# Hybrid attention and gating trunk: gating's output products moved behind attention, one PSUM sum per token tile and column half

## Chip, cores and metric

The kernel runs on one core of one Trainium2 chip. The metric is the device time of one execution in microseconds (us), as the median of several runs. All engines of the core work at once: PE (matrix products; PEld is its weight load), DVE (VectorE), ACT (ScalarE), POOL (GpSimd) and SP (SyncE, which here only issues DMAs).

## What is computed

Two layers over 512 latent and 256 context tokens with 1024 features. The change lies in layer 0, the hybrid layer. There a normalised and modulated input `h` is projected to q, k, v (8 heads of 64) and to u, g of a spatial gating unit (512 features). The mixer's output is one product over 1024 features, of which 512 come from attention and 512 from gating:

```python
q, k, v, u, g = jnp.split(h_lat @ w_in, splits, axis=-1)
a_lat = neighbourhood_attention(heads(q), heads(k), heads(v), heads(kc), heads(vc), rpb)
s_lat = spatial_gating(jax.nn.gelu(u), jax.nn.gelu(g), w_s, b_s)
y_lat = jnp.concatenate([a_lat, s_lat], axis=-1) @ w_out
```

The same is done for the context tokens. The result is normalised (RMS), gated and added to the input; a second norm and modulation make the input of the gated MLP (ConvFFN). Layer 1 has retention in place of the hybrid mixer and a second FFN.

## The kernel before

Tokens are six tiles of 128: tiles 0 to 3 are latent, 4 and 5 context, and they are worked on in the order 4, 5, 0, 1, 2, 3 (`toks`). Every fp32 product is three fp32r matmuls on split operands (`mm3`, L128): `split` (L97) lets ACT make the high part and DVE the low part. A weight unit is 128 x 1024 (512 KB): `unit` (L101) loads it into one of three raw buffers (tag `raw`) and splits it into one of the places that `slot` hands out in turn. PSUM has eight banks of 512 columns: four with tag A, two with B and two with C (L94).

The order of instructions on each engine is made by a planner, which takes program order as its guide and moves ready work forward. Where `self.fixed` names an engine (L73, L62), its instructions stay in program order; in the opening these are PE and SP ("TQ", L708), the others are planned.

Stages of layer 0, with the names the trace shows:

- Opening (`sgu`, L708 to L766). `first_load` loads x (`xn`), `ada_first` (L176) the modulation weights of a quarter of the features (`ar`; products `ad`, turned by `adt` into columns `ab`). `first_x` (L411) computes the first norm of each tile and scales it, `first_xT` (L1731) transposes it (`ht` to `xT`, copied by ACT), `first_h` (L1741) applies the modulation and splits into `h0a` and `h1a`. `tokens(q, ...)` are the gating products (`ug`) of one quarter of the features (`ug10` to `ug13` are their weights).
- Gating (L772 to L829). The second half of the projection (`ug00` to `ug03`), the mixing over positions (`mix`), the transposes (`turn`, tiles `st0A` to `st3C`, split into `sT`), then four weight units `wos0` to `wos3` and the output products `wsg`: `out_pieces` (L588) makes 12 pieces (six tiles, two column halves of 512) of 12 matmuls each, and ACT copies each sum into `y` (name `ysg`). Background jobs (`bg`, modulation gates, tiles `ag` and `G`) are called in between.
- Attention (L831). Four pairs of heads; each pair has its projection (`project_pair`, tiles `pq`, `px`, `pk`, `pv`, `py` from weights `wq`, `wk`, `wv`), scores `s`, softmax on DVE and ACT (`sc`), transposes `pt`, and the products `o` and `oc` with the values, which end in `at`. The projection of the next pair runs as `fills`, one per step. In the last pair the fills are two pieces of the output product of tile 4 with the features of pairs 0 and 1 (`woa0`, `woa1`; `wata`). `bias_tiles` loads each head's bias (`slab`) and makes `tm`.
- End of attention (L884 to L897). The weights `woa2`, `woa3`; then `watb` (tile 4 with pairs 2 and 3, 12 matmuls) and `watc` (the other five tiles with all four pairs, 12 matmuls per half). DVE adds each sum to `y`. After a tile's second half, `final` calls `residual` (L425): squares (`jyb`, ACT), times the gate `G` (DVE), the root (POOL), plus the input (`xb`), squares (`jxb`), root, scaling. Then the next stage's blocks are built: transposes `ht`, `sa` (tiles 4, 5, 0) and `sb` (tiles 1, 2, 3), splits `hb` and `b`. The FFN's first products are `pf`; `pf000b` is the first on the second half's blocks.
- The FFN writes partial outputs by DMAs from POOL's queue (`yp`, `ypg` to `yd`, later `yf`).

`h0` and `h1` are tags of two SBUF places of 24 KB per partition: the high and low part of `h` until the last projection, then blocks of the FFN and (`h1`) its staging tile `sa`.

Of the kernel before, what the change touches and what calls it, by code (L numbers as in the profile page):

```python
# [18 lines left out]
KD = 8  # L19
# [49 lines left out]
class Trunk:  # L69
# [106 lines left out]
    def ada_first(self, q, pool, tag):  # L176
# [6 lines left out]
        for n in range(2):  # L183
            for kp in range(2):
# [226 lines left out]
    def first_x(self, toks, xn):  # L411
        V, G = self.V, self.G
        for t in toks:
            y = xn[t]
            junk = self.bp.tile([P, D], BF16, name=f"jx{t}", tag="t2k", bufs=4)
            ss = self.bp.tile([P, 1], F32, name=f"ssx{t}", tag="ss", bufs=8)
            if t % 2:
                V.tensor_tensor_reduce(
                    out=junk, in0=y, in1=y, scale=1.0 / D, scalar=0.0, op0=ALU.mult, op1=ALU.add, accum_out=ss
                )  # L420
            else:
                self.S.activation(junk, y, AF.Square, scale=1.0 / 32, accum_out=ss)
            V.tensor_scalar(out=y, in0=y, scalar1=self.rstd(ss, f"x0{t}"), scalar2=None, op0=ALU.mult)

    def residual(self, t, y, gate, src, last, name, xt):  # L425
# [58 lines left out]
    def alloc_blocks(self, l):  # L484
# [5 lines left out]
        self.sa = self.bp.tile([P, KD, n], F32, name=f"sa{l}", tag="h1", bufs=1)  # L490
# [133 lines left out]
    def finisher(self, gates, src, ab, name, xts, last=False, mlp=None):  # L624
# [4 lines left out]
        def fin(t, y):  # L629
# [12 lines left out]
            self.residual(t, y, gates[1 if t >= 4 else 0], src(t), last, name, xt)  # L642
# [19 lines left out]
    def sgu(self, y, xn):  # L662
        S, V, T, G, a = self.S, self.V, self.T, self.G, self.a
        toks = (4, 5, 0, 1, 2, 3)
        with ExitStack() as ctx:
# [17 lines left out]
            with ExitStack() as c2:  # L683
# [29 lines left out]
                later = self.ada_first(1, fp, "B")  # L713
                raws[1] = ug_raw(1)
                for i in range(4):
                    product(i)
                self.first_x((4, 5), xn)
                turned(0)
                turn()
                product, turn = later  # L720
                self.first_h(0, 2, xT)
                w = ug_split(0, raws[0])
                self.first_x((0, 1), xn)
                tokens(0, (4, 5))
                turned(1)
                product(0)
                product(1)
                self.first_x((2, 3), xn)
                self.first_h(0, 0, xT)
                turned(2)  # L730
                product(2)
                product(3)
                tokens(0, (0, 1))
                self.first_h(0, 1, xT)
                turn()
                tokens(0, (2, 3))
                def after(q):
                    u = ug_split(q, raws[q])
                    for chunk, ct in chunks:
                        self.first_h(q, chunk, xT)  # L740
                    return u

                w = after(1)
                product, turn = self.ada_first(2, fp, "B")
                raws[2] = ug_raw(2)
                for n, t in enumerate(toks):
# [4 lines left out]
                    if n == 1:  # L751
                        turn()
                        w2 = after(2)
# [6 lines left out]
                for n, t in enumerate(toks):  # L760
                    tokens(2, (t,))
                    if n == 0:
                        turn()
                        w3 = after(3)
# [6 lines left out]
            st = [sp.tile([P, 4, 768], F32R, name=f"sT{i}", tag=f"sT{i}") for i in range(2)]  # L771
# [30 lines left out]
            def turn(half):  # L802
                for f in (2 * half, 2 * half + 1):
                    for tt, tag in (((0, 1, 2, 3), "A"), ((4, 5), "C")):
                        n = len(tt) * P
                        pt = self.ps(f"st{f}{tag}", tag)
                        fc = slice(f % 2 * P, f % 2 * P + P)
                        for j, t in enumerate(tt):
                            T.transpose(pt[:, j * P : (j + 1) * P], u[half][:, t, fc], self.ident)
                        c = slice(tt[0] * P, tt[0] * P + n)  # L810
                        self.split(st[0][:, f, c], st[1][:, f, c], pt[:, :n])
# [12 lines left out]
            wo = [self.unit(a["hyb_out"][(4 + f) * P : (5 + f) * P], f"wos{f}") for f in range(4)]  # L824
            mix(1)
            turn(1)
            pieces = self.out_pieces([(st[0][:, f, :], st[1][:, f, :]) for f in range(4)], wo, y, toks, True, None, "sg")
            for f in pieces:
                f()  # L829

    def attention(self, y, final):  # L831
        a = self.a
        with ExitStack() as ctx:
# [15 lines left out]
            toks = (4, 5, 0, 1, 2, 3)  # L849
            for i in range(n + lag + 1):  # L850
                if i < n:
# [3 lines left out]
                    if step == 0:  # L855
                        pr["at"] = [ap.tile([P, 768], F32R, name=f"at{x}{j}", tag=f"at{x}", bufs=4) for x in range(2)]
                        if j == 3:
                            A = (
                                [pairs[0]["at"], pairs[1]["at"]],
                                [self.unit(a["hyb_out"][f * P : (f + 1) * P], f"woa{f}") for f in (0, 1)],  # L860
# [1056 lines left out]
```

## Time and profile before

| | |
|---|---|
| time, three runs | 1894.61, 1899.68, 1899.76 us (median 1899.68) |
| profiled execution | 1894.09 us, of which the span of the trace is 1892.3 |
| mean granted PE clock | 0.979 |
| opening and gating | 0 to 157.7 us |
| attention, to the last projection | 157.7 to 322.2 |
| last pair of heads | 322.2 to 360.9 |
| output products and norm | 360.9 to 400.3, then 400.3 to 419.3 |
| FFN of layer 0 and layer 1 | 419.3 to the end |
| DMA | 249.80 MB, mean 132 GB/s over the span |

The bounds of the stages are read from the first and last start of their tiles. In a table of stretches, each row has the stretch, its length, then for PE, PEld, DVE, ACT and POOL the busy time with the count of instructions, and last the granted PE clock (1.00 is full speed), the DMA engines' busy share and GB/s. In a timeline a row is: start, duration, engine, line, operation, output<-inputs, shapes, count, and in brackets the idle time before it and what ended it; all rows say L61, the helper that records every instruction, so tiles tell the place. A matmul's duration contains the pipeline's latency; the spacing of starts is what it costs PE. In a list of waits: who waited for whom, the sum, how often, and the longest, in us.

### The profile page before, as it was taken

How to read it: one execution, taken by the hardware profiler on the slowest of the kernel's cores; microseconds unless marked ns; L12 is line 12 of the kernel's file. 1: busy time of each engine (PE TensorE's matmuls, PEld its weight loads, DVE VectorE, ACT ScalarE, POOL GpSimd, SP SyncE). 2: the span in 40 equal slices, each digit the busy share in tenths (PEclk: the TensorE clock that was granted, in tenths of full speed). 3: DMA queues.
4: the chain of work that ended last, by engine and by line, in shares of the span. 5: the costliest groups of instructions: out<-in, count | busy, mean ns of one | idle time of the engine just before them, and what ended most of it. 6: DMA issues, size and time to landing. Idle time of an engine off the chain costs nothing. (4 is left out here: it accounts for less than half of the span.)

```text
span 1892.3 us, 28961 instructions
## 1 busy us (share of the span) xinstructions
PE 1796.2 (95%) x11104; PEld 1596.4 (84%) x11104; DVE 1328.8 (70%) x2250; ACT 1015.1 (54%) x1828; POOL 320.6 (17%) x451
## 2 busy tenths in 40 slices
PE   6999999879999999999889999999999989999997
PEld 4887777669989889998779989988999779899996
DVE  4532545779877878778777566676655689888987
ACT  4523455766646466565565434343444467576763
POOL 1102212120122222222121011011001110122221
PEclk9999999979999999999999999999999989999999
DMA  8323323232667768677642322431421225777772
GB/s 310 127 89 95 95 93 95 72 115 84 193 165 151 186 137 179 149 166 153 228 153 86 118 80 83 123 101 53 126 68 60 98 77 149 180 200 177 193 176 101
DMA packets 83628, 249.80 MB, mean 132 GB/s; under 512 B 10912, under 2 KB 12448, under 8 KB 83488
## 3 DMA queue, kind: packets, MB, share of 16 engines
q1 hardware_dynamic: 56960, 199.00, 32.2%
q0 software_dynamic: 25952, 48.83, 15.1%
q8 instruction: 87, 1.43, 0.3%
q14 instruction: 53, 0.43, 0.1%
q10 hardware_dynamic: 576, 0.11, 0.0%
HBM read 191.28 MB, written 39.85 MB: 122 GB/s over the span
## 5 line engine op out<-in xcount | busy, mean ns | idle before, releaser
L61 DVE SCALAR_TENSOR_TENSOR cv<-pre,cw,cv 128x769 f32<-128x769 f32 (+1 forms) x176 | 152.7, 881 | 7.7 <-ACT cv L61 7.1
L61 DVE SCALAR_TENSOR_TENSOR acc<-ar,cs,acc 128x512 f32<-128x512 f32 x160 | 118.1, 750 | 27.7 <-DMA ar<-in_adaw 18.1
L61 ACT ACTIVATE cv<-pre,cw 128x770 f32<-128x770 f32 (+1 forms) x88 | 81.1, 924 | 37.9 <-DVE pre L61 37.3
L61 POOL DMA_DIRECT2D yf<-yp x64 | 55.6, 869 | 261.9 <-ACT yp L61 159.0
L61 POOL DMA_DIRECT2D yd<-yp x54 | 46.5, 868 | 186.1 <-ACT yp L61 182.6
L61 ACT COPY yp<-wf 128x512 f32<-128x512 f32 x118 | 67.9, 577 | 17.6 <-PE wf L61 17.3
L61 ACT ACTIVATE pre<-px 128x256 f32<-128x256 f32 (+2 forms) x160 | 54.3, 366 | 40.0 <-PE px L61 39.6
L61 POOL DMA_DIRECT2D yd<-ypg x54 | 44.7, 850 | 158.4 <-ACT ypg L61 150.1
L61 POOL TENSOR_SCALAR rrr<-rmv 128x2 f32<-128x2 f32 x16 | 3.0, 190 | 360.9 <-DVE rmv L61 360.9
L61 ACT ACTIVATE g<-cv 128x770 fp32r<-128x770 f32 (+1 forms) x44 | 32.5, 738 | 29.8 <-DVE cv L61 29.7
L61 PE MATMUL px<-hs,wd 128*128 128x384 f32 x240 | 45.3, 336 | 0.0
L61 PEld LDWEIGHTS px<-hs,wd 128*128 128x128 f32 x240 | 42.4, 188 | 1.6
L61 ACT ACTIVATE pre<-py 128x384 f32<-128x384 f32 (+1 forms) x40 | 17.4, 436 | 44.5 <-DVE cv L61 28.2
L61 DVE TENSOR_TENSOR g<-cv,g 128x770 fp32r<-128x770 f32 (+1 forms) x44 | 36.2, 822 | 6.8 <-ACT g L61 6.2
L61 ACT ACTIVATE cv<-cv 128x770 f32<-128x770 f32 (+1 forms) x44 | 32.7, 742 | 12.3 <-DVE cv L61 12.1
L61 DVE TENSOR_TENSOR cv<-cv 128x770 f32<-128x770 f32 (+1 forms) x44 | 36.2, 823 | 2.4 <-ACT cv L61 1.4
L61 DVE TENSOR_TENSOR pre<-pre,pz 128x256 f32<-128x256 f32 (+1 forms) x60 | 20.9, 372 | 23.2 <-PE pz L61 23.2
L61 PE MATMUL ad<-ar,c 128*32 128x256 f32 (+1 forms) x224 | 26.7, 515 | 10.4 <-DMA ar<-in_adaw 9.8
L61 DVE CUSTOM_DVE_ANT_0 sc<-s,tm 128x256 f32<-128x256 f32 x32 | 13.4, 420 | 32.6 <-PE s L61 23.5
L61 ACT ACTIVATE sc<-sc,sst 128x512 f32<-128x512 f32 x32 | 23.2, 725 | 23.1 <-DVE sc L61 20.7
L61 PEld LDWEIGHTS px<-hs 128*128 128x128 f32 x240 | 30.8, 190 | 5.5 <-DVE pre L61 4.5
L61 POOL TENSOR_TENSOR tm<-slab,mask 128x256 f32<-128x256 f32 (+1 forms) x32 | 24.4, 793 | 65.2 <-DVE sst L61 65.0
(2617 smaller groups left out, 6852.9 us busy)
## 6 DMA issues: line engine op xcount, KB each, us to landing
ar<-in_adaw SPq DMA_DIRECT2D x96, 512.0 KB, 4.2
yf<-yp POOLq DMA_DIRECT2D x64, 256.0 KB, 4.1
yd<-yp POOLq DMA_DIRECT2D x54, 256.0 KB, 5.1
yd<-ypg POOLq DMA_DIRECT2D x54, 256.0 KB, 4.6
fin<-xd SPq DMA_DIRECT2D x10, 512.0 KB, 7.4
xd<-xd SPq DMA_DIRECT2D x8, 512.0 KB, 3.2
xn<-in_x SPq DMA_DIRECT2D x6, 512.0 KB, 6.2
xb<-in_x SPq DMA_DIRECT2D x6, 512.0 KB, 3.6
```

What stands on the lines that cost most here:

```text
L61: r = f(*p, **k)
```

## The change

The gating unit makes no output product any more. Its transposed and split result is kept per token tile (`sT`, in the place `y{t}`). In attention, `part(t, n, fs)` adds the features `fs` (0 to 3 gating, 4 to 7 attention) for tile `t` and half `n` to one PSUM sum of tag A. Five weight units (`wo0` to `wo4`) are loaded at the last pair, three of them into the place of `h1`; twelve fills do features 0 to 4 of tiles 4 and 5. After attention `wo5` to `wo7` are loaded into places of attention's tiles (`unit_parts` is new), then each tile's sums are finished and `final` reads them in PSUM. So the copies of `wsg` and the adds of `wata`, `watb` and `watc` are gone. The staging tile `sa` gets a place of its own, and the scratch for DMAs issued by GpSimd is given as 4096 bytes to make room.

```diff
+    def unit_parts(self, src, name, pool, tags):
+        raw = self.bp.tile([P, 1024], F32, name=f"{name}r", tag="raw", bufs=3)
+        self.load(raw, src)
+        p = [pool.tile([P, 512], F32R, name=f"{name}{g}", tag=g, bufs=1) for g in tags]
+        for h in range(2):
+            self.split(p[2 * h], p[2 * h + 1], raw[:, 512 * h : 512 * h + 512])
+        return [Halves([p[i], p[2 + i]]) for i in range(2)]
...
     def residual(...)
+        if sums is None:
+            sums = [y[:, h] for h in hv]
         for n, h in enumerate(hv):
-            self.ssq(y[:, h], f"y{name}{t}", n)
-        for h in hv:
-            V.tensor_tensor(out=y[:, h], in0=y[:, h], in1=gate[:, h], op=ALU.mult)
+            self.ssq(sums[n], f"y{name}{t}", n)
+        for n, h in enumerate(hv):
+            V.tensor_tensor(out=y[:, h], in0=sums[n], in1=gate[:, h], op=ALU.mult)
...
-        self.sa = self.bp.tile([P, KD, n], F32, name=f"sa{l}", tag="h1", bufs=1)
+        self.sa = self.bp.tile([P, KD, n], F32, name=f"sa{l}", tag="sa", bufs=1)
...
             def turn(half):
-                for f in (2 * half, 2 * half + 1):
-                    for tt, tag in (((0, 1, 2, 3), "A"), ((4, 5), "C")):
...
+                for tt, tag in (((4, 5), "C"), ((0, 1), "B"), ((2, 3), "C")):
+                    pt = self.ps(f"st{half}{tt[0]}", tag, (P, 2, 2, P))
+                    for i, t in enumerate(tt):
+                        if half == 0:
+                            pool = self.bp if t < 4 else self.lp
+                            self.sT[t] = pool.tile([P, 2, 4, P], F32R, name=f"sT{t}", tag=f"y{t}", bufs=1)
+                        for f in range(2):
+                            T.transpose(pt[:, i, f, :], u[half][:, t, f * P : f * P + P], self.ident)
+                        fs = slice(2 * half, 2 * half + 2)
+                        self.split(self.sT[t][:, 0, fs, :], self.sT[t][:, 1, fs, :], pt[:, i])
...
-            wo = [self.unit(a["hyb_out"][(4 + f) * P : (5 + f) * P], f"wos{f}") for f in range(4)]
             mix(1)
             turn(1)
-            pieces = self.out_pieces([(st[0][:, f, :], st[1][:, f, :]) for f in range(4)], wo, y, toks, True, None, "sg")
-            for f in pieces:
-                f()
...
     def attention(self, y, final):
+            wo, sums = [], {}
+            row = lambda f: a["hyb_out"][(f + 4) % 8 * P : ((f + 4) % 8 + 1) * P]
+            def part(t, n, fs):
+                if fs[0] == 0:
+                    sums[t, n] = self.ps(f"wo{t}{n}", "A")
+                o = slice(512 * n, 512 * n + 512)
+                for f in fs:
+                    if f < 4:
+                        x = [self.sT[t][:, i, f, :] for i in range(2)]
+                    else:
+                        x = [z[:, self.gcol(t)] for z in pairs[f - 4]["at"]]
+                    self.mm3(sums[t, n], x, [z[:, o] for z in wo[f]], f == 0, f == 7)
...
                         if j == 3:
-                            A = (...)
-                            fills = self.out_pieces(*A, y, toks[:1], False, None, "ata", "A")
+                            home = self.bp.tile([P, 6, 1024], F32R, name="woh", tag="h1", bufs=1)
+                            for f in range(5):
+                                at_ = None if f < 2 else (home[:, 2 * f - 4], home[:, 2 * f - 3])
+                                wo.append(self.unit(row(f), f"wo{f}", at_))
+                            fills = [
+                                lambda t=t, n=n, fs=fs: part(t, n, fs)
+                                for t in toks[:2]
+                                for n in range(2)
+                                for fs in ((0, 1), (2, 3), (4,))
+                            ]
...
+            spare = ap.tile([P, 2, 1024], F32R, name="wo7s", tag="ptall")
+            wo.append(self.unit_parts(row(5), "wo5", ap, ("q0", "q1", "kb0", "kb1")))
+            wo.append(self.unit_halves(row(6), "wo6", ap, "sc", 4))
+            wo.append(self.unit(row(7), "wo7", (spare[:, 0], spare[:, 1])))
             self.early()
-            self.out_group(*B, y, toks[:1], False, final, "atb", "A")
-            self.out_group(A[0] + B[0], A[1] + B[1], y, toks[1:], False, final, "atc", "A")
+            for t in toks:
+                for m in range(2):
+                    part(t, m, range(5, 8) if t > 3 else range(8))
+                y[t] = self.ytile(t, "yat")
+                final(t, y[t], [sums[t, m] for m in range(2)])
...
-    nc = bacc.Bacc("TRN2", target_bir_lowering=False, num_devices=1)
+    nc = bacc.Bacc("TRN2", target_bir_lowering=False, num_devices=1, dynamic_dma_scratch_size=4096)
```

The opening is written in another order, and all five engines keep program order in it: `self.fixed` is "TQSVG" (PE, SP, ACT, DVE, POOL). `first_x` is divided into `first_sq` (sum of squares and root) and `first_scale`. Every second copy of `first_xT` goes to DVE. x of tiles 0 and 1 is loaded ahead of the modulation weights, and the first gating weight between their halves (`amid`):

```diff
-                self.fixed = "TQ"
-                product, turn = self.ada_first(0, fp, "C")
                 self.first_load((0, 1), xn)
-                raws = {0: ug_raw(0)}
+                product, turn = self.ada_first(0, fp, "C", lambda: later.update(w=ug_raw(0)))
                 self.first_load((2, 3), xn)
...
+                sq(4, "S")
+                sq(5, "V")
+                scale(4)
+                scale(5)
+                sq(0, "S")
+                sq(1, "V")
+                turned(0)
+                scale(0)
+                scale(1)
+                product(0)
+                product(1)
+                w = ug_split(0, raws[0])
+                turned(1)
+                product(2)
+                product(3)
+                turn()
+                self.first_h(0, 2, xT)
+                sq(2, "S")
+                self.first_h(0, 0, xT)
+                sq(3, "V")
+                scale(2)
+                scale(3)
+                tokens(0, (4, 5))
+                turned(2)
+                product, turn = ada1
+                for i in range(4):
+                    product(i)
+                self.first_h(0, 1, xT)
+                tokens(0, (0,))
+                turn()
+                w1 = ug_split(1, raws[1])
+                tokens(0, (1, 2, 3))
...
-                    if n == 1:
+                    if n == 2:
                         turn()
-                        w2 = after(2)
+                        w2 = ug_split(2, raws[2])
+                        after(2)
```

More of the change, by code (lines that the diff above doesn't have):

```diff
@@ L174, in ada_unit_src, with ada_first @@
         return self.a["adaw"][r : r + P]
-    def ada_first(self, q, pool, tag):
+    def ada_first(self, q, pool, tag, amid=None):
         S, V, T = self.S, self.V, self.T
@@ L183, in ada_first @@
         for n in range(2):
+            if n and amid:
+                amid()
             for kp in range(2):
@@ L409, in first_load, with first_sq, first_scale, residual @@
             self.load(xn[t], self.a["x6"][t * P : (t + 1) * P])
[L411 to L425, printed above, removed]
+    def first_sq(self, t, xn, engine):
+        y = xn[t]
+        junk = self.bp.tile([P, D], BF16, name=f"jx{t}", tag="t2k", bufs=4)
+        ss = self.bp.tile([P, 1], F32, name=f"ssx{t}", tag="ss", bufs=8)
+        if engine == "V":
+            self.V.tensor_tensor_reduce(
+                out=junk, in0=y, in1=y, scale=1.0 / D, scalar=0.0, op0=ALU.mult, op1=ALU.add, accum_out=ss
+            )
+        else:
+            self.S.activation(junk, y, AF.Square, scale=1.0 / 32, accum_out=ss)
+        return self.rstd(ss, f"x0{t}")
+    def first_scale(self, t, xn, r):
+        self.V.tensor_scalar(out=xn[t], in0=xn[t], scalar1=r, scalar2=None, op0=ALU.mult)
+    def residual(self, t, y, gate, src, last, name, xt, sums=None):
         V = self.V
@@ L627, in finisher, with fin @@
         state = {"n": 0}
-        def fin(t, y):
+        def fin(t, y, sums=None):
             if not done and not last:
@@ L641, in fin @@
                 state["n"] += 1
-            self.residual(t, y, gates[1 if t >= 4 else 0], src(t), last, name, xt)
+            self.residual(t, y, gates[1 if t >= 4 else 0], src(t), last, name, xt, sums)
             done[t] = y
@@ L706, in turned @@
                     self.first_xT(*chunks[n], xn, fp, xT, banks[n])
-                self.fixed = "TQ"
-                product, turn = self.ada_first(0, fp, "C")
+                self.fixed = "TQSVG"
+                r, later = {}, {}
                 self.first_load((0, 1), xn)
-                raws = {0: ug_raw(0)}
+                product, turn = self.ada_first(0, fp, "C", lambda: later.update(w=ug_raw(0)))
                 self.first_load((2, 3), xn)
-                later = self.ada_first(1, fp, "B")
+                raws = {0: later["w"]}
@@ L718, in sgu @@
-                turned(0)
+                self.first_h(0, 1, xT)
+                tokens(0, (0,))
                 turn()
[L720 to L736, printed above, removed]
+                w1 = ug_split(1, raws[1])
+                tokens(0, (1, 2, 3))
                 def after(q):
-                    u = ug_split(q, raws[q])
                     for chunk, ct in chunks:
                         self.first_h(q, chunk, xT)
-                    return u
-                w = after(1)
+                after(1)
@@ L763, in sgu @@
                         turn()
-                        w3 = after(3)
+                        w3 = ug_split(3, raws[3])
+                        after(3)
                 w = w3
@@ L770, in sgu @@
             vl = sp.tile([P, 6, 512], F32R, name="vnl", tag="vnl")
-            st = [sp.tile([P, 4, 768], F32R, name=f"sT{i}", tag=f"sT{i}") for i in range(2)]
             for t in toks:
@@ L1738, in first_xT @@
                     self.T.transpose(pt[:, i, j * P : (j + 1) * P], xn[t][:, k * P : (k + 1) * P], self.ident)
-            self.S.copy(xT[chunk][:, 2 * kk : 2 * kk + 2, :], pt)
+            if kk % 2:
+                self.V.tensor_copy(xT[chunk][:, 2 * kk : 2 * kk + 2, :], pt)
+            else:
+                self.S.copy(xT[chunk][:, 2 * kk : 2 * kk + 2, :], pt)
     def first_h(self, q, chunk, xT):
@@ L1758, in build @@
         self.sst = {}
+        self.sT = {}
         self.jobs = []
```

25 lines of the change are left out of this document (5 added, 20 removed).

## Prediction

> **What bounds the kernel.** I read the busy shares first, then who TensorE (PE) waited for up to 425 us, then the busy table of the stretches that the change touches.
>
> ```profile
> PE 1796.2 (95%) x11104; PEld 1596.4 (84%) x11104; DVE 1328.8 (70%) x2250; ACT 1015.1 (54%) x1828; POOL 320.6 (17%) x451
> PE ad L61 <- DMA ar<-in_adaw: 9.8, 4, 8.1
> PE ht L61 <- DVE ysg L61: 7.8, 2, 4.2
> PE ug L61 <- ACT h0a L61: 5.4, 1, 5.4
> ...
> 120.00:157.70 37.70, 36.90 (x160) 28.45 (x158) 7.43 (x12) 12.04 (x20) 0.00 (x0) 1.00 0.22 75
> 157.70:322.20 164.50, 157.62 (x984) 124.82 (x983) 80.40 (x226) 83.60 (x193) 35.06 (x47) 0.98 0.33 105
> 322.20:360.90 38.70, 32.46 (x248) 24.70 (x247) 29.14 (x102) 29.74 (x77) 3.67 (x5) 1.00 0.14 42
> 360.90:400.30 39.40, 35.79 (x170) 28.96 (x168) 28.16 (x47) 23.47 (x55) 9.31 (x16) 0.96 0.38 133
> 400.30:419.30 19.00, 10.54 (x50) 8.91 (x47) 13.59 (x24) 11.91 (x30) 7.16 (x13) 0.68 0.35 118
> ```
>
> PE is the bound: 95% busy, and in every stretch but the last its column is nearly the length of the stretch. So a moved matmul saves nothing by itself. The change can win only idle PE time: matmuls put where PE now waits, and waits that go. The table shows where. In the gating end (120 to 157.7) PE is full, while VectorE (DVE, 7.43) and ScalarE (ACT, 12.04) rest. Near the end of attention (322 to 361) PE has 38.70 - 32.46 = 6.2 us of holes. After it come the output products (361 to 400) and a tail to the next stage's first matmul on its second half (400 to 419), where PE is busy for 10.5 of 19 us, at a granted clock of 0.68, and waits for DVE and ACT, which run the norm of the last tokens.
>
> **Term 1, the gating end.**
>
> ```profile
> 120.31 0.48 PE L61 MATMUL wsg<-wos0h,sT 128*128 128x512 f32 x1
> ...
> 120.86 0.60 PE L61 MATMUL st3A<-ident,un 128*128 128x128 f32 x4
> ...
> 121.43 0.70 PE L61 MATMUL wsg<-wos0h,sT 128*128 128x512 f32 x2
> ...
> 129.72 0.50 PE L61 MATMUL wsg<-wos0h,sT 128*128 128x512 f32 x1 [0.22 <-ACT ysg L61]
> ...
> 157.73 0.41 PE L61 MATMUL pq<-h0a,wq0h 128*128 128x512 f32 x1
> 156.53 1.06 ACT L61 ACTIVATE wq0h<-wq0r 128x1024 fp32r<-128x1024 f32 x1 [0.80 <-PE wsg L61]
> 157.62 1.23 DVE L61 TENSOR_TENSOR wq0l<-wq0r,wq0h 128x1024 fp32r<-128x1024 f32 x1 [28.31 <-ACT wq0h L61]
> ```
>
> There are 12 pieces (6 token tiles, 2 halves) of 12 matmuls (4 features, 3 products) = 144. The last 10 pieces run from 129.72 to 157.73: 28.01 / 120 = 0.2334 us each, so 144 are 33.6 us. The whole stretch is 157.73 - 120.31 = 37.4 us. In it stay the last transposes (120.86 to 121.43, 0.6 us) and four gate products of the background job, about 1.0 us by the spacing of their neighbours. That removes 35.8. Attention's first products must then start near 122 us. Their weight takes the two splits shown (1.06 and 1.23); today its slot comes free only behind the output weights, tomorrow behind the gating weights, while the mixing products still run. I charge 1.1 us of wait (0 if the splits are ready, 4 if two units' splits queue on DVE behind the mixing). **-34.7** (-35.8 to -31.8). The 12 ACT copies that go, and the finer splits of the gating result (128x256 in place of 128x512), lie on engines idle here and are costed at nothing. If DVE were not idle, six more small splits would be some 2 us.
>
> **Term 2, the last pair of heads.** The fills grow from 2 pieces of 6 matmuls to 12 pieces with 60: five weight units for two tiles and two halves. 48 more at 0.2334 are 11.2 us of PE work.
>
> ```profile
> 321.96 0.28 PE L61 MATMUL py<-h1a,wv3h 128*128 128x256 f32 x1
> ...
> 299.75 0.33 SPq L61 DMA_DIRECT2D woa3r<-in_hyb_out  x1
> 311.42 0.63 SPq L61 DMA_DIRECT2D slab<-in_rpb  x1
> L61 POOL TENSOR_TENSOR tm<-slab,mask x32: 510/859/1567, 167.3 to 330.4; 128x256 f32<-128x256 f32 x16, 128x128 f32<-128x128 f32 x16
> ```
>
> Three of the five units (wo2 to wo4) go to the place of h1, which the projection reads until 322. So they cannot be split earlier, and their raw copies hold all three raw buffers until then. SyncE's queue would stand at the next weight load, and behind it may stand the last head's bias load (now at 311.42) and the FFN's first weight; today GpSimd makes the last tiles from it at 330.4, so a load some microseconds after 322 is still in time. The splits, 3 x 1.06 on ACT and 3 x 1.23 on DVE, come into a stretch where these engines are already busy for about 29 of 39 us and softmax passes from one to the other. Lower end: all 6.2 us of holes filled, +5.0. Upper end: nothing filled and the splits in series, 11.2 + 6.9 = +18.1. I take half of the holes, **+8.0**: the fills depend on nothing but weights, so they can run in the waits, but PE takes its queue in order.
>
> **Term 3, the output products.**
>
> ```profile
> 360.92 0.47 PE L61 MATMUL watb<-woa2h,at 128*128 128x512 f32 x1
> ...
> 367.50 0.39 PE L61 MATMUL watc<-woa0h,at 128*128 128x512 f32 x1
> ...
> 375.67 0.27 PE L61 MATMUL ht<-ident,ysg 128*128 128x128 f32 x1
> 379.56 1.52 PE L61 MATMUL ht<-ident,ysg 128*128 128x128 f32 x7 [3.61 <-DVE ysg L61]
> ...
> 388.34 1.04 PE L61 MATMUL ht<-ident,ysg 128*128 128x128 f32 x8
> 389.14 0.47 PE L61 MATMUL watc<-woa0h,at 128*128 128x512 f32 x1
> ...
> 399.46 0.85 PE L61 MATMUL watc<-woa3s,at 128*128 128x512 f32 x3
> ...
> 419.25 0.69 PE L61 MATMUL pf000b<-b,wp0h 128*128 128x384 f32 x1 [1.63 <-ACT b L61]
> ```
>
> Today 132 matmuls; afterwards 2 tiles x 2 x 9 = 36 and 4 tiles x 2 x 24 = 192, so 228. The 36 from 367.50 to 375.67 take 0.227 each: 51.7 us. Four groups of transposes (0.80 each, 388.34 to 389.14) add 3.2 and attention's last products 0.6. One wait of 1.0 is allowed: the open sums of tiles 4 and 5 hold all four banks of tag A, so tile 0 starts only when tile 4's first half is read. Together 56.5, against 39.4 now, in which the hole of 3.6 us should go: a tile now occupies PE for 48 x 0.227 = 10.9 us, about as long as its norm chain takes. **+17.1** (+16.1 without the wait; +22.8 if the hole stays, with about 2 us of slow matmuls after it). The third more weight (wo5) at the end is 0.7 us of DVE and 0.6 of ACT per half; its places (q0 to kb1) come free with the last scores, before the last products, and it is costed at nothing; uncovered it is 2.3.
>
> **Term 4, the tail.** DVE loses the adds and the norm reads the sums where they are.
>
> ```profile
> L61 DVE TENSOR_TENSOR ysg<-watc,ysg 128x512 f32<-128x512 f32 x8 | 5.5, 683 | 0.0
> L61 DVE TENSOR_TENSOR ysg<-ysg,G 128x512 f32<-128x512 f32 x8 | 5.5, 690 | 1.8 <-ACT jyb L61 1.6
> L61 ACT ACTIVATE jyb<-ysg 128x512 bf16<-128x512 f32 x9 | 5.6, 626 | 4.0 <-DVE ysg L61 4.0
> ...
> 408.27 0.61 ACT L61 ACTIVATE jyb<-ysg 128x512 bf16<-128x512 f32 x1
> ```
>
> An operand in PSUM costs nothing extra: the add reads PSUM in 683 ns, the multiply reads SBUF in 690. Two adds per tile go, 1.4 us of DVE. More important, DVE and ACT are two tiles behind when the last matmul is issued at 400 (the last tile's second sum of squares starts at 408.27) and will not be, since PE becomes the slower one. From 408.27 to 419.25 the chain of one tile takes 11.0; with the first half's square 11.6, in place of 419.25 - 400.3 = 18.9. **-7.3** (0 if the backlog stays, -8.5 with the saved multiply wait).
>
> The Trainium skill speaks against holding sums: PSUM — Partial Sum Buffer, section Summary: rules for kernel authors, says to evacuate promptly since PSUM is tight. By it this change would stall PE; that is rival (c) below. The trace of before reads each sum once, so it shows no such hold.
>
> **Term 5, the opening.**
>
> ```profile
> 15.00:20.00 5.00, 3.31 (x17) 3.04 (x15) 1.48 (x5) 4.13 (x7) 0.57 (x2) 1.00 1.03 419
> ...
> 23.71 0.79 PE L61 MATMUL ug<-ug10h,h0a 128*128 128x512 f32 x1 [5.40 <-ACT h0a L61]
> ...
> 41.93 0.39 PE L61 MATMUL ug<-ug11h,h0a 128*128 128x512 f32 x1
> ...
> 47.93 0.66 PE L61 MATMUL adt<-ident,mr 128*128 128x128 f32 x4 [0.71 <-ACT mr L61]
> ```
>
> DMA is full (419 GB/s, 1.25 us per 512 KB tile). Three tiles move ahead of the second half of the first modulation weights, which so come 3.8 us later; but the second chunk's transposes now run before that, in the 5.4 us hole. By hand I get the first gating product no earlier than now, a cold spell less, then a hole of up to 3 us before the third chunk's transposes, as VectorE, ScalarE and GpSimd wait in program order. The second quarter's products (41.93) then start about 1 us earlier, and the 0.7 us wait at 47.93 goes with the later turn. **-2** (-5 to +5).
>
> The sa tile's own place and the smaller DMA scratch are costed at nothing: no wait on h1 is listed at the start of either FFN; the scratch is the second rival.
>
> **Sum** against the profiled execution's 1894.09 us (span 1892.3): -34.7 + 8.0 + 17.1 - 7.3 - 2.0 = -18.9, so 1875.2. The runs shown before are 1894.61, 1899.68 and 1899.76, so the median lies 5.6 above the profiled one and the lowest 0.5. I add half the median's distance, 2.8: **1878**.
>
> **Rivals.** (a) *All holes fill*: terms at their good ends, -35.8 + 5.0 + 16.1 - 8.5 - 5 = -28, so 1866 to 1869. For it: DVE and ACT idle where they are charged. Against: in-order PE, late wo2 to wo4.
> (b) *The change doesn't do what it says*, the work moves and no hole fills: -34.7 + 18.1 + 22.8 + 0 - 2 = +4, so 1901. For it: the splits enter the softmax stretch. Against: fills are independent of softmax.
> (c) *Banks*: the norm holds each sum for two squares and two multiplies (about 3 us), and if PE had to wait it out for all six tiles, 18 us: 1896. Against: four banks are two tiles, 11 us of matmuls, so only the first handover should show.
> (d) *Slower*: the scratch for DMA issued by GpSimd is cut from its default to 4096.
>
> ```profile
> yd<-yp POOLq DMA_DIRECT2D x54, 256.0 KB, 5.1
> ...
> 566.38 0.86 POOL L61 DMA_DIRECT2D yd<-yp  x1 [8.10 <-ACT yp L61]
> 567.78 0.85 POOL L61 DMA_DIRECT2D yd<-yp  x1 [0.55 <-ACT yp L61]
> ...
> PE wf L61 <- ACT ypg L61: 4.6, 2, 3.2
> ```
>
> Transfers are issued 1.4 us apart and land after 5.1. If two no longer fit, the second waits 3.7 us. Over 54 such transfers that is 200 us on GpSimd; four buffers hide most, and if a sixth reaches PE (which already waits 4.6 us for ypg) it is +33: 1911. It decides from the point where two transfers don't fit; nothing in the trace shows the limit.
>
> **Chances.** Forecast 0.58 (1869 to 1888), (a) 0.20, (b) 0.10, (c) 0.05, (d) 0.07. A measurement of this kernel tells 0.3% from no change, 5.7 us around 1899.68: forecast and (a) are faster, 0.78; (b) and (c) the same, 0.15; (d) slower, 0.07. The range is 1865 to 1896: it takes in (a) to (c)'s edge and leaves out (b) and (d) and a little below.
>
> **What would show it.** Attention's first projection near 120 to 124 us; the last pair longer by about 8 us and with fewer PE holes; four output tiles about 11 us apart, without a hole of 3 us; 11 to 12 us from the last output product to the FFN's second-half product. Wrong, if PE waits for wo weights or for norm reads of the sums, if the last head's bias comes late, or if the wf products wait longer for yp and ypg.

## The result, and the profile after

The changed kernel takes **1871.61 us** (median of 4 runs, 1862.28 to 1876.50) against 1898.62 (4 runs, 1894.61 to 1899.76): a ratio of 0.9856, 95% interval 0.981 to 0.9901. Two later sets, each beside runs of the kernel before on the same chip, gave 0.9858 (0.9836 to 0.988) and 0.9865 (0.9851 to 0.9879). In microseconds the medians differ by 27.0, 27.5 and 24.9. The profiled execution is the one of 1875.21 us; its span is 1873.4.

The page of after, the line of busy times:

```profile
PE 1792.3 (96%) x11104; PEld 1596.5 (85%) x11104; DVE 1327.4 (71%) x2247; ACT 1009.4 (54%) x1815; POOL 318.8 (17%) x451
```

PE has as many instructions as before and 4 us less busy time. What the kernel won is 15 us of idle PE time in this pair of executions. The table of stretches shows where (columns: length, then busy time and instructions of PE, weight loads, DVE, ACT and POOL, then granted clock, DMA share, GB/s). After:

```profile
36.84:116.00 79.16, 79.16 (x553) 65.09 (x551) 37.70 (x73) 34.31 (x60) 8.46 (x16) 1.00 0.35 120
116.00:281.00 165.00, 159.96 (x1004) 126.40 (x1003) 82.88 (x235) 85.62 (x199) 35.14 (x47) 0.98 0.35 109
281.00:322.00 41.00, 40.41 (x272) 30.14 (x272) 32.63 (x104) 31.93 (x80) 4.77 (x5) 1.00 0.25 75
322.00:381.30 59.30, 58.80 (x282) 47.43 (x279) 29.43 (x46) 28.80 (x67) 8.67 (x20) 1.00 0.33 111
381.30:393.00 11.70, 8.34 (x52) 6.92 (x50) 7.89 (x15) 9.01 (x21) 3.79 (x9) 0.96 0.39 132
```

The last pair of heads (281 to 322) now has 0.6 us of PE holes where it had 6.2, the output products (322 to 381.3) have 0.5 where they had 3.6, and the tail is short, at a clock of 0.96 instead of 0.68: by the marks below 10.0 us in place of 19.1 (pf000b starts 1.7 us before the last row ends). The marks between the stages, from the timeline of after (start, duration, engine, operation):

```profile
113.51 0.44 PE L61 MATMUL mx<-vnh,sguwh 128*128 128x384 f32 x1
...
115.96 0.48 PE L61 MATMUL pq<-h0a,wq0h 128*128 128x512 f32 x1
...
323.08 0.66 PE L61 MATMUL pt<-ident,sc 128*128 128x128 f32 x4
...
381.24 1.03 PE L61 MATMUL ht<-ident,yat 128*128 128x128 f32 x8
...
391.26 0.44 PE L61 MATMUL pf000b<-b,wp0h 128*128 128x384 f32 x1 [1.77 <-ACT b L61]
```

The same marks of before, from its timeline, as far as the prediction doesn't show them:

```profile
117.52 0.44 PE L61 MATMUL mx<-vnh,sguwh 128*128 128x384 f32 x1
...
360.50 0.66 PE L61 MATMUL pt<-ident,sc 128*128 128x128 f32 x4
...
400.15 0.38 PE L61 MATMUL ht<-ident,ysg 128*128 128x128 f32 x2
```

Set against each other, the front of the kernel adds up as follows. "Mixing" is the first mixing product of the second half, "projection" the last of attention's projections on `h1a` (321.96 before, 280.00 after), "last tile" the transposes that end the output products.

| stage, between marks | before | after | difference | predicted |
|---|---|---|---|---|
| start to mixing (term 5) | 117.52 | 113.51 | -4.0 | -2 |
| mixing to attention's first product (1) | 40.2 | 2.45 | -37.8 | -34.7 |
| to the last projection | 164.2 | 164.0 | -0.2 | 0 |
| to pt of the last head tile (2) | 38.5 | 43.1 | +4.5 | +8.0 |
| to the last tile (3) | 39.65 | 58.16 | +18.5 | +17.1 |
| to pf000b (4) | 19.1 | 10.0 | -9.1 | -7.3 |
| **sum at pf000b** | 419.25 | 391.26 | **-28.0** | -18.9 |
| from pf000b to the end | 1473.05 | 1482.1 | +9.1 | 0 |

The two spans differ by 18.9 us, exactly the predicted sum. That is a coincidence: the front won 9 us more than predicted and the part behind it lost 9. The experiments had two questions: is this loss the change's, and why is the front better?

### The profile page after: what moved, and what is told of

It reads as the page before. It is cut to its first block, busy times and chain, and to the rows that moved or that the text cites. A ratio compares the mean times of both kernels' runs of the same rounds, so it can differ in the third digit from the quotient of the medians.

```text
span 1873.4 us, 28952 instructions
## 1 busy us (share of the span) xinstructions
PE 1792.3 (96%) x11104; PEld 1596.5 (85%) x11104; DVE 1327.4 (71%) x2247; ACT 1009.4 (54%) x1815; POOL 318.8 (17%) x451
## 5 line engine op out<-in xcount | busy, mean ns | idle before, releaser
L61 PE MATMUL px<-hs 128*128 128x256 f32 x240 | 33.9, 293 | 7.1 <-DVE pre L61 7.1
L61 DVE TENSOR_TENSOR pre<-pre,pz 128x256 f32<-128x256 f32 (+1 forms) x60 | 21.0, 374 | 27.5 <-PE pz L61 27.2
L61 ACT ACTIVATE cv<-cv 128x770 f32<-128x770 f32 (+1 forms) x44 | 32.8, 745 | 13.2 <-DVE cv L61 13.0
```

Of the source, the lines that this page charges most:

```text
L61: r = f(*p, **k)
```

## The experiments

**1. The changed kernel again (a_again), unaltered.**

> The changed kernel once more, unaltered, with fresh runs of the kernel before beside it. In the first two traces the front of the kernel, up to the first feed-forward product on the second half (pf000b), is 28.0 us earlier with the change, and the 1473 us behind it took 9.1 us longer. Theory A (what is lost behind the front is not the change: PE stops and clock dips that fall differently in each run): the front is again at 391 to 392 us, the part behind it differs from 1482 by some microseconds, and the median lies 22 to 30 us under the kernel before. Theory B (a lasting cost of the change in the feed-forward stages, the smaller scratch or another order of work): the part behind the front is again 1480 to 1484 us, and its extra time sits at the same places in both feed-forward stages.

1871.94 us (5 runs, 1867.24 to 1875.56). The front ends at 389.75, and the part behind it took 1475.75 us, 6 less than in the first trace of the same program. That speaks for A, though the front missed A's 391 to 392 by 1.3 us. But a further set (a_again2, below) gave 391.48 and 1483.1, inside B's range, so these traces alone don't decide it; runs 11 and 12 take it up again.

**2. The smaller scratch alone (b_scratch).**

```diff
-    nc = bacc.Bacc("TRN2", target_bir_lowering=False, num_devices=1)
+    nc = bacc.Bacc("TRN2", target_bir_lowering=False, num_devices=1, dynamic_dma_scratch_size=4096)
```

> The kernel before with the change's smaller scratch (4096) for GpSimd's DMAs and nothing else. Rival (d) (transfers wait for scratch, and a few waits reach PE): 5 us or more over the kernel before, with the 9.1 us found behind the front in the first traces as its likely size (about 1908), and longer waits of the wf products on ypg. Theory A (the scratch holds what is needed): within 3 us of the kernel before, and the time from a yd transfer's issue to its landing stays near 5.1 us.

1897.85 us (12 runs) beside 1899.4 (17 runs), ratio 0.9989 (0.9975 to 1.0004). The transfers, from the list of DMA issues of this run (last number: median us from issue to landing), and its PE waits between 453 and 910 us:

```profile
yd<-yp POOLq DMA_DIRECT2D x54, 256.0 KB, 5.2
```

```profile
PE wf L61 <- ACT ypg L61: 5.2, 2, 3.2
```

5.2 us to landing against 5.1, 5.2 us of waits on ypg against 4.6: a transfer that had to wait for scratch would land 3.7 us later by the prediction's estimate. Rival (d) falls.

**3. The old opening in the changed kernel (a_oldopen).** `first_x`, the "TQ" order and the copies of `first_xT` are those of before; the rest is after.

```diff
-                self.fixed = "TQSVG"
+                self.fixed = "TQ"
...
-                sq(4, "S")
-                sq(5, "V")
+                for i in range(4):
+                    product(i)
+                self.first_x((4, 5), xn)
...
```

> The changed kernel with the opening of the kernel before (its order of loads, squares, transposes and gating products); the output products stay moved. If the opening's gain is real and adds to the rest, as the traces have it: 4 us longer than the changed kernel (about 1876), the first mixing product at 117 to 118 in place of 113.5 us, and attention's first product still 2.4 us behind it. Rival, the opening is hidden by a later wait or is noise: within 1.5 us of the changed kernel.

1875.10 us (6 runs), 3.2 more than the changed kernel in the same set. The timeline of this run:

```profile
116.59 0.44 PE L61 MATMUL mx<-vnh,sguwh 128*128 128x384 f32 x1
```

Mixing starts 3.1 us later than in after, attention's first product (119.05) again 2.46 behind it, and pf000b comes at 394.83, 3.4 to 5.1 later than in three traces of the changed kernel. The times alone don't separate the two kernels (ratios to before 0.9877, 0.9854 to 0.99, and 0.9858, 0.9836 to 0.988). By the marks the opening is worth 3 to 5 us by itself and hides nothing else.

**4. No list of fills (a_nofill).** The pair of heads gets no fills; tiles 4 and 5 make their whole sums afterwards.

```diff
+                            fills = []
...
-                    part(t, m, range(5, 8) if t > 3 else range(8))
+                    part(t, m, range(8))
```

> The changed kernel, but no output product runs beside the last pair of heads: the 60 products of tiles 4 and 5 on the first five units come after attention, with the rest of their sums. Theory (the 60 products fill some 6 us of PE holes that the softmax of the last pair leaves): the last pair shortens by 60 x 0.2334 - 6 = 8 us, the output products lengthen by 14 us, and the whole is 5 to 7 us longer than the changed kernel. Rival (PE is slowed by the fills as much as they save, since softmax passes the same engines as their weight splits): within 1.5 us of the changed kernel. By the prediction's middle value, half the holes: 3 us longer.

1870.26 us (5 runs), 1.7 less than the changed kernel (ratios 0.9853 and 0.9858, so no difference). By the times alone the rival would have won. The groups of PE instructions of this run between 277 and 319.2 us, while the last pair of heads still ran, say otherwise (count, then busy us and mean ns):

```profile
L61 PE MATMUL wo<-woh,sT 128*128 128x512 f32 x18 | 5.4, 406 | 0.0
L61 PE MATMUL wo<-woh,at 128*128 128x512 f32 x9 | 3.3, 425 | 0.0
L61 PE MATMUL wo<-wo1h,sT 128*128 128x512 f32 x6 | 2.6, 435 | 0.0
L61 PE MATMUL wo<-wo0h,sT 128*128 128x512 f32 x6 | 2.5, 412 | 0.0
L61 PE MATMUL wo<-wo5q,at 128*128 128x512 f32 x6 | 2.1, 439 | 0.0
```

With three smaller groups these are 54 output products in the last pair although program order has none there: the planner moved them forward itself. The experiment removed the list, not the fills, and so tested neither theory. The next two hold the order fast.

**5 and 6. PE in program order, with fills (a_pin) and without (a_pin_nofill).** In both PE keeps program order from the last pair to the end of the output products; the second also has the edit of a_nofill.

```diff
                         if j == 3:
+                            self.fixed = "T"
...
                 final(t, y[t], [sums[t, m] for m in range(2)])
+            self.fixed = ""
```

> The changed kernel with PE held to program order from the last pair of heads to the end of the output products (the 60 fills stand one piece to a step there). It is the partner of the next run; by itself it asks what the planner's moves are worth in this stretch: the stretch from attention's last projection to the FFN's second-half product was 111 us in both profiles of the changed kernel. If the fills written by hand are enough to fill the holes: 111 to 114 us. If the planner's own moves do the filling: 116 us or more.

> PE held to program order as in the run before, and no output product beside the last pair of heads: all 60 stand behind attention, where the planner cannot bring them forward. (In the unpinned version without the list of fills the trace showed output products between the heads all the same: the planner had moved them.) Theory (holes of the softmax, some 6 us in the kernel before, are filled by these products and by nothing else): the last pair is 38 to 40 us long with PE busy for about 33, and the stretch to the FFN's second-half product is 5 to 8 us longer than in the run with fills held in order. Rival (the fills save nothing, PE only queues up elsewhere): within 1.5 us of it.

a_pin 1884.82 us (4 runs), a_pin_nofill 1893.49 (10 runs). Their tables of stretches, for the last pair of heads, the output products and the tail; with fills:

```profile
279.43:326.77 47.34, 41.98 (x285) 32.32 (x284) 32.38 (x105) 32.98 (x80) 4.51 (x5) 0.93 0.23 67
326.77:393.20 66.43, 61.55 (x272) 49.89 (x272) 29.48 (x46) 28.75 (x67) 8.62 (x20) 0.95 0.27 96
393.20:403.90 10.70, 8.13 (x53) 7.05 (x51) 6.20 (x12) 7.30 (x18) 3.78 (x9) 1.00 0.48 155
```

and without:

```profile
280.92:325.71 44.79, 33.15 (x234) 25.15 (x232) 31.94 (x105) 32.84 (x80) 4.52 (x5) 0.85 0.23 71
325.71:403.60 77.89, 73.01 (x322) 59.35 (x322) 29.50 (x46) 28.86 (x67) 8.62 (x20) 0.96 0.24 82
403.60:414.30 10.70, 8.17 (x52) 7.03 (x50) 6.12 (x12) 7.25 (x18) 3.78 (x9) 1.00 0.47 155
```

Without fills the pair has 44.79 - 33.15 = 11.6 us of holes. The 51 products that run in it with fills, 11.9 us of work, make it only 2.6 us longer; the holes shrink to 5.4. From the last projection to pf000b the stretch is 124.4 us with fills and 133.4 without: **9.0 us** for the fills. The rival (within 1.5 us) falls. The theory has the cause right and two sizes wrong: it expected 5 to 8 us for the fills, and 38 to 40 us for the pair without them, which took 44.8. The kernel before took 38.5 us there with 12 products in the pair, so the weight splits or the fixed order make holes that before did not have; no run separates the two. 6.2 of the 9.0 us are holes filled in the pair. Most of the other 2.8 can be put down to the clock, 0.85 against 0.93 there (an estimate from the busy times: 33.15 x 0.15 - 41.98 x 0.07 = 2.0 us), since a PE that waits more also runs slower afterwards, as the last section shows.

The planner's order beats the fills written by hand by 124.4 - 111.2 = 13.2 us, as the second guess for a_pin had it (116 us or more). Only about 4 of these are in the last pair (47.3 against 43.1 us). About 9 are in the output products (66.4 against 57.5 us up to the last of them): there a_pin waits 2.0 us before attention's last products (`oc`) and 2.9 before a tile's transposes (`ht`), has six products more, and starts products 0.43 us apart after each of the two waits. The tail is 10.7 us in both of these runs, as in after.

**7 and 8. Two sums (a_twosums), or one sum copied out at once (a_evac).** In a_twosums the gating part and the attention part have banks of their own, ACT copies the first to SBUF, DVE adds the second:

```diff
-                    self.mm3(sums[t, n], x, [z[:, o] for z in wo[f]], f == 0, f == 7)
+                    self.mm3(sums[t, n], x, [z[:, o] for z in wo[f]], f % 4 == 0, f % 4 == 3)
+                if fs[-1] == 3 and n == 1:
+                    y[t] = self.ytile(t, "yat")
+                    for m in range(2):
+                        self.S.copy(y[t][:, 512 * m : 512 * m + 512], sums[t, m])
+                if fs[-1] == 7:
+                    self.V.tensor_tensor(out=y[t][:, o], in0=sums[t, n], in1=y[t][:, o], op=ALU.add)
...
```

In a_evac the sum stays one, and the norm reads a copy:

```diff
+                for m in range(2):
+                    self.S.copy(y[t][:, 512 * m : 512 * m + 512], sums[t, m])
-                final(t, y[t], [sums[t, m] for m in range(2)])
+                final(t, y[t])
```

> The changed kernel with the products where the change puts them, but with two PSUM sums for each tile and half: the gating part is copied to SBUF by ACT, the attention part added to it by DVE, and the norm reads SBUF, as in the kernel before. Theory (what was won is the place of the products; DVE has time for the two adds of 0.68 us per tile, since a tile occupies PE for 11 us): the front up to pf000b is 0.7 to 2 us longer than the changed kernel's 390 to 391, all of it in the tail behind the last product. Rival (the shorter tail comes from the adds that left DVE, which without the one sum is behind again): 5 to 7 us longer, with the tail back at 15 us or more.

> The changed kernel with one sum per tile and half, but ACT copies it to SBUF as soon as it is complete and the norm reads the copy: the bank is free after about 0.6 us instead of after two squares and two multiplies. By the rule to evacuate promptly (rival (c)): PE waits less for banks, a gain of up to 3 us at the first handover and more where later ones wait. Theory (no wait is there to win, since the traces show none at a handover): no gain; the tail is longer by the copies of the last tile, so the front up to pf000b 0.6 to 1.3 us longer than the changed kernel's.

a_twosums 1875.92 us, a_evac 1875.74 (4 runs each; ratios to before 0.9872, 0.984 to 0.9903, and 0.9872, 0.9833 to 0.991). The totals can't tell these from the changed kernel, so I read the marks. From the start of the last three output products to pf000b: before 19.79 us, after 10.71, a_twosums 11.46, a_evac 11.46. From the last projection to pf000b: after 111.3 (111.2 in the next two traces), a_twosums 114.7, a_evac 112.6. The table of stretches of a_twosums, output products and tail:

```profile
323.84:383.00 59.16, 56.33 (x261) 44.93 (x260) 35.76 (x57) 33.41 (x75) 11.11 (x20) 1.00 0.33 108
383.00:394.50 11.50, 8.48 (x53) 6.99 (x51) 8.01 (x15) 7.12 (x18) 4.27 (x9) 1.00 0.38 131
```

With the adds back, DVE is busy for 35.8 of 59.2 us, so it is not the bound and is not behind at the end: the tail grows by 0.75 us, not by 5 to 7. The rival falls. The extra time, 3.4 us in all, is larger than the 0.7 to 2 expected, and only 0.75 of it is in the tail; 2.8 us of PE waits stand inside the output products (1.2 behind attention's copy `pcT` on ACT, 1.6 behind the block sums `sa` on DVE), where the changed kernel has 0.5.

Copying the sums out at once gained nothing: 1.4 us more, half of it in the tail. In the timeline of after, the last product of tile 5 and the first of tile 0, which needs a bank that tile 4 held:

```profile
332.81 0.85 PE L61 MATMUL wo<-wo7s,at 128*128 128x512 f32 x3
333.49 0.40 PE L61 MATMUL wo<-wo0h,sT 128*128 128x512 f32 x1
```

Three products at 0.227, and no wait. The one wait of 1.0 us that term 3 allowed isn't there, and of the 0.5 us that PE waits in the whole stretch none is for a bank; rival (c) falls with it. The rule to evacuate promptly (the Trainium skill, PSUM — Partial Sum Buffer, section Summary: rules for kernel authors) finds no wait to remove at this place, because tile 4's norm has finished with its banks (its last multiply ends at 331.0 us) while tile 5 still occupies PE.

**9 and 10. More places for the FFN's partial products (a_yp8), beside the changed kernel (a_again2).** This was my guess at what spreads the time behind the front.

```diff
                     tiles = [fp.tile([P, 2 if first else 4, 512], F32, name=f"yp{l}", tag="yp")]
...
+                    tiles.append(self.bp.tile([P, 4, 512], F32, name=f"ypx{l}", tag="sa", bufs=1))
                     parts.extend(t[:, i] for t in tiles for i in range(t.shape[1]))
```

> The changed kernel with eight instead of four places for the FFN's partial products on their way to memory (yp): the four new ones take the place sa, which the change gave to the block sums alone and which is dead once these are made. Theory (the spread behind the front, 1439 to 1450 us from fo00h to the end in six profiles, is PE waiting for a copy to yp or ypg, whose place a GpSimd DMA still holds, and the lower clock after each such wait): the waits of wf on yp and ypg, 5.7 us in both traces of the changed kernel before fo019h, go; the time falls by 6 to 15 us, to 1857 to 1866, and the runs of this kernel lie closer together. Rival (those waits are followed by others, on pre or on the DMAs themselves): within 3 us of the changed kernel.

> The changed kernel unaltered, on the same chip as the run before, for a direct comparison; 1868 to 1876 us by the earlier runs, the stretch from the last projection to the FFN's second-half product 111.2 us.

a_yp8 1873.30 us (5 runs, ratio 0.984, 0.9826 to 0.9854); a_again2 1877.47 (4 runs, 0.9865, 0.9851 to 0.9879). The intervals overlap by a hair, so whether the 4.2 us are a gain is unclear. The theory falls in any case. The PE waits of a_yp8 from 423 to 960 us:

```profile
PE wf L61 <- ACT ypg L61: 5.2, 2, 3.2
...
PE wf L61 <- ACT yp L61: 1.1, 1, 1.1
...
PE wf L61 <- ACT ypx L61: 0.6, 1, 0.6
```

6.9 us with eight places, 7.2 in a_again2 with four. The copy isn't late for want of a place. What makes it late at one place is read in the first trace of after, on DVE, ACT and PE in turn (in brackets: idle time before, and who ended it):

```profile
611.71 0.75 DVE L61 SCALAR_TENSOR_TENSOR acc<-ar,cs,acc 128x512 f32<-128x512 f32 x1 [2.69 <-DMA ar<-in_adaw]
...
613.02 1.03 ACT L61 ACTIVATE cv<-pre,cw 128x770 f32<-128x770 f32 x1 [5.71 <-DVE pre L61]
613.96 1.05 ACT L61 COPY ypg<-wf 128x512 f32<-128x512 f32 x2
...
614.58 0.79 PE L61 MATMUL wf<-fo06h,g 128*128 128x512 f32 x1 [3.42 <-ACT ypg L61]
```

A tile of modulation weights lands late. DVE, in order, stands at it; the `pre` sums behind it come late; ACT stands at `cv` for them, with the copies to ypg behind; PE waits 3.42 us for a bank. The releaser that the wait names is the last link of four. I did not try an edit at the first one.

**11 and 12. The kernel before, twice more (b_again, b_again2).**

> The kernel before, unaltered, to see its part behind the front more often. Behind fo00h the first trace of before took 1439.6 us (448.6 of them up to fo019h), the three traces of the unaltered changed kernel 1444.0 to 1452.5 (452.8 to 456.4). If that difference is chance (loads of modulation weights that land late for DVE at other places in each run): 1443 us or more here too, 452 or more up to fo019h. If the change costs there: 1437 to 1442, 447 to 450 up to fo019h.

> The same once more: by chance 1443 us or more behind fo00h, by a cost of the change 1437 to 1442. The front up to pf000b 419 to 421 us in either case.

One run each, 1902.09 and 1903.87 us. Here fo00h and fo019h are the ACT splits of the first FFN's first and twentieth output weight; fo02h is the third one's.

| trace | pf000b | pf000b to end | fo00h to end | of it to fo019h | fo02h to end |
|---|---|---|---|---|---|
| before | 419.25 | 1473.1 | 1439.6 | 448.6 | 1415.7 |
| b_again | 420.54 | 1479.8 | 1446.8 | 450.3 | 1423.1 |
| b_again2 | 421.02 | 1481.1 | 1447.4 | 448.3 | 1423.7 |
| after | 391.26 | 1482.1 | 1450.1 | 456.4 | 1423.9 |
| a_again | 389.75 | 1475.7 | 1444.0 | 452.8 | 1417.3 |
| a_again2 | 391.48 | 1483.1 | 1452.5 | 454.5 | 1426.6 |

By the whole length chance is right: the first trace of before was 7 us faster behind the front than the other two, and that made most of the 9.1. From pf000b to the end the two kernels' values overlap. By the part up to fo019h neither guess is clean: 448 to 450 without the change, 453 to 456 with it. 2.0 to 3.0 us of that lie between fo00h and fo02h, and there it is the mark that moved: fo00h is split 30.6 to 32.1 us behind pf000b with the change and 32.9 to 33.7 without, while from pf000b to fo02h the values overlap (56.6 to 58.5 against 56.7 to 57.4), and from fo02h to fo019h by a hair (426.1 to 430.2 against 424.6 to 426.6). b_scratch, without the move, had 453.6 up to fo019h, and a_oldopen, with both the move and the scratch, 449.2, so neither explains the rest alone. On the mean of three traces the front is 29.4 us shorter and the part behind it 2.4 us longer, but that part spreads by 7 to 8 us within each kernel; the medians differ by 25 to 27.5. **Whether up to 4.5 us are given back behind the front, or nothing, is left open.**

## Why the prediction was right, and which terms were off

The forecast was 1878, the range 1865 to 1896, the result 1871.61: faster, by the mechanism named, and by 8 us more than the sum. Each term has the sign that was forecast and is off by 1.4 to 3.5 us; four of the five are off to the same side, so that the errors at pf000b add up to 9 us. Point by point:

**Term 1** (-34.7, measured -37.8). The step was right, the size short: "I charge 1.1 us of wait". There was none. The timeline of after, on ACT:

```profile
111.70 1.06 ACT L61 ACTIVATE wq0h<-wq0r 128x1024 fp32r<-128x1024 f32 x1 [1.52 <-DMA wq0r<-in_hyb_qkv]
```

The first attention weight is split 1.8 us before mixing starts, so the good end of my own bounds was due. Most of the other 2 us are the last transposes and the gate products that I had kept in the stretch (1.6 by the prediction's count): they run beside attention's first products, in a stage that did not become longer (164.0 against 164.2).

**Term 2** (+8.0, measured +4.5) is the step that failed: "I take half of the holes". All of them were filled. 57 of the 60 products ran inside the pair; 45 more than before are 10.5 us of work, and the pair grew by 4.5. The argument against, that PE takes its queue in order, forgot that the planner chooses that order and sets single products between the heads' steps; with the order held fast, in run 5, 5.4 us of holes stay. Runs 5 and 6 show both halves: 51 of the same products save 9.0 us even in a fixed order, and the planner's order is worth about 4 more in this pair. The fear for wo2 to wo4 was empty: ACT split the three from 280.3 to 284.0 us, right behind the last projection, DVE from 281.4 to 289.4, and PE had wo0 and wo1 to begin with, from 285.35. The last head's bias tile was begun at 291.6, in time.

**Term 3** (+17.1, measured +18.5). The hole of 3.6 us went, as said, and the wait for a bank did not come. The sum of its parts was off in another place: 58.2 us against 56.5. The 231 products (three were left over from the pair) take 54.7 us, 0.237 each with 0.5 us of waits in it, where 228 were charged at 0.227, 51.7 in all. The missing wait (1.0) and the transposes, of which only three groups lie between these marks (2.45 against 3.2), give part of the 3.0 back.

**Term 4** (-7.3, measured -9.1). The mechanism is the one named: DVE and ACT are no longer behind when PE ends. Run 7 separates it from the fused sum, which is worth 0.75 us of it. The size was short because the chain of one tile, charged with the 11.0 us that it took before, takes 9.8 now. Its last transposes start 0.21 us apart before, at the clock of 0.68, and 0.11 after, at 0.96; the first root takes POOL 0.79 us before and 0.30 after, for a reason that no run shows. The last tile's second square, from the timeline of after on ACT:

```profile
381.50 0.60 ACT L61 ACTIVATE jyb<-wo 128x512 bf16<-128x512 f32 x1 [3.16 <-PE wo L61]
```

From 381.50 to pf000b at 391.26 are 9.76 us. ACT had been idle for 3.16 us when the sum came, so nothing is queued ahead. That an operand in PSUM costs nothing extra holds for the multiply, from the groups of DVE instructions between 322 and 393 us:

```profile
L61 DVE TENSOR_TENSOR yat<-wo,G 128x512 f32<-128x512 f32 x12 | 8.3, 690 | 14.8 <-ACT jyb L61 10.2 <-PE wo L61 4.6
```

690 ns, as before from SBUF.

**Term 5** (-2, measured -4.0): the sign was right, and run 3 puts 3.1 of it down to the opening's own edits.

**The rivals.** (a) had the front right, -28, if not term by term (term 3 came to +18.5, not +16.1), and its 1866 to 1869 missed the median by 2.6 us; with 0.20 it was rated too low. (b) is refuted by the table of stretches, (c) by run 8, (d) by run 2. The prediction had every effect behind the front at nothing; the traces don't show whether that holds to better than 4.5 us.

**The signs.** Attention's first projection came at 115.96 us (120 to 124 expected), the pair grew by 4.5 us (about 8), the output tiles are 11.9 us apart without a hole of 3, and pf000b follows 10.7 us behind the start of the last three output products (11 to 12). Of the signs of being wrong none came: PE waits for no weight `wo` and no norm read, and from pf000b to fo019h the wf products wait 5.7, 5.7 and 7.2 us for yp and ypg in the three traces of the changed kernel, against 6.2, 5.5 and 5.1 in the three of before.

## What to carry to other kernels

Where PE is the bound, work that needs only weights should be placed where PE waits for other engines, and if the order on PE is free to interleave single matmuls, such holes can fill in full, as they did here; in a fixed order about half of them filled. A tail is short when the engines behind PE have caught up before its last matmul, so making PE the slower side near the end was worth more here (most of 9.1 us) than trimming the chain (0.75). Before two spans are compared, compare the stages: the same program varied by 8.5 us behind the front, more than the forecast was off by in all (6.4).

## What the hardware showed unexpectedly

A single wait of 3.42 us on PE cost about 6.5 us of its time. The table of stretches of after around the wait shown in run 9 (the clock is the third number from the end):

```profile
610.00:615.00 5.00, 1.58 (x8) 1.26 (x7) 3.29 (x5) 1.98 (x3) 0.18 (x1) 0.89 0.26 107
615.00:620.00 5.00, 5.00 (x15) 4.42 (x15) 3.71 (x6) 3.22 (x7) 2.19 (x3) 0.50 0.81 118
620.00:625.00 5.00, 5.00 (x26) 4.65 (x25) 3.12 (x4) 1.39 (x4) 0.23 (x1) 0.92 0.84 238
```

After the wait, matmuls of 128x512 start 0.43 us apart (615.17, 615.60, 616.02) where 0.233 is usual, and the clock is back only in the next five microseconds. From 615 to 620 PE is "busy" all the time and gets 15 matmuls done, where the next five microseconds get 26. At a clock of 0.50, and 0.92 after it, about 3 us are lost on top of the wait (an estimate: 5 x 0.50 + 5 x 0.08 = 2.9). Busy time hides this; the clock column shows it. The Trainium skill, TensorE: Matmul & The Clock Gate, section Part 1: The HAM clock gate (the "warmup" mystery), gives half the clock after an idle window of about 3.4 us, and 426.7 ns between the starts of matmuls of 512 columns at that clock, measured on bf16. The trace agrees with the spacing, 0.43 us. The wait is as long as that window, but the clock of 0.89 in the first row means 1.1 us at half the clock before 615, so it fell at about 613.9, some 2.7 us after PE went idle. That makes a late DMA dear. It may be why runs of one program lie 14 us apart (1862.28 to 1876.50) with the same instructions; no run here showed that alone.
